# A hand-built instruction list for a convolution layer: a clock for all its DMA transfers, two late block loads held back, and the list built anew

## The chip, the cores and the metric

The kernel runs on one core of one Trainium2 chip. A core has a matrix engine (TensorE, PE in the profile, whose weight loads have a row of their own, PEld), a vector engine (VectorE, DVE), an activation engine (ScalarE, ACT), a general engine (GpSimd, POOL) and an engine that only issues DMA transfers (SyncE, SP). Each engine works off its own list of instructions in the order of the program, and the engines wait for one another by semaphores. The metric is the device time of one execution in microseconds (us): the median of several runs of the kernel before was 1088.61 us, from 1088.28 to 1089.37.

## The reference, cut to what matters

Two layers over 128 context tokens and 512 sample tokens (640 in all, width 1024), each `x + gate * mixer(modulated norm of x)`; shift, scale and gate come from a product of a condition vector with a large matrix (`ada_w`). Layer 0 is a convolution branch and layer 1 a state-space branch. The change concerns layer 0:

```python
m = jax.nn.silu(cond) @ w + b                       # shift, scale, gate of a layer
h = rms_norm(y, g) * (1.0 + sc) + sh
u = h @ w_in + b_in                                 # 1024 -> 3 * 2048
a, a_gate, z = jnp.split(u, 3, axis=-1)
v = a * jax.nn.sigmoid(a_gate)
v = depthwise_conv(v, w_dw, b_dw)                   # 31 taps along rows of 64
v = jax.nn.silu(layer_norm(v, ln_g, ln_b))
out = (v * jax.nn.silu(z)) @ w_out                  # 2048 -> 1024
y = y + gate * out
```

## The kernel before

**Tiles.** Channels lie on the 128 partitions and the 640 tokens along them. `u` has 48 tiles of 128 channels: 16 each of `a`, `g` (the gate) and `z`. One tile is 48 matmuls (three for each of 8 blocks of the inner dimension and each half of the tokens, since a float32 product is made from a high and a low part of both operands). `PLAN0` (line 42) gives the order in which PE makes the tiles after the opening, in which `g0`, `a0` and `g1` are made. Tile `i` of the convolution starts when `g i` has gone through the sigmoid on ACT (`after_g`, line 642) and `a i` has been multiplied with it on DVE (`after_a`, line 654) into `v i`, which lies in one of four buffers. PE's result lies in one of two PSUM buffers (`mm`), which come free when ACT or DVE has read them.

**The convolution** of a tile is 31 taps. `NPOOL[i]` (line 43) of them are multiplied by ACT (`late_taps`, line 828, into three buffers `tp`) and added by POOL (`seam_sums`, line 842); the centre tap is the first write of ACT (`init`, line 791); the rest run on DVE, one instruction a tap (`conv`, line 799). POOL also forms, by a product and four sums (lines 855 to 865), the tap products that cross the seam of the two token halves. When a tile is done, ACT squares it (`square`, line 699), and PE's column sums of tile and square go into the spare columns of the PSUM buffer of a later tile (`side_sums`, line 715), from where DVE adds them up (`add_sums`, line 727). After all 16 tiles come the statistics (`stats`, line 880, and `means`, line 896), the normalising on DVE (`normalise`, line 911), the gate (`gate_z`, line 923) and the products with `w_out` (`out_pass`, line 944).

**Weights.** Each tile needs 512 KB. SP loads them as `wf` (two buffers; `weights`, line 391); ACT rounds them into a high part `wh` and writes its negative into `wl` (`split`, line 402); a second load, issued by POOL, adds the weights from memory onto `wl` as it lands, so that `wl` is the low part. So each tile costs two transfers, one on SP's queue and one on POOL's. `wh` and `wl` have three buffers each.

**Late blocks.** Of the 24 blocks of the condition's matrix, 16 are loaded in the course of layer 0 (`blocks`, line 688): four transfers of 256 KB each, on SP. PE multiplies a block ahead of a certain `g` tile (its host) into spare columns of that tile's PSUM buffer (`lead_of`, line 634), ACT copies the row out behind the tile's sigmoid (`row_copy`, line 627), and PE turns it behind the matching `a` tile (`ada_turn`, line 129). Block 0 goes with `g2`, block 1 with `g3`. From block 2 on, a block waits until block `n - 2` has been multiplied.

**The list.** None of these orders is written by hand. While the program is built, the class `Order` (line 244) plays the layer through: every generator above is a chain of steps "engine, duration, instruction", every buffer a ring with the time at which it comes free. At each step it takes, over all chains and engines, the one that could begin first by its own clocks (ties go by the priorities of `PRIO0`, line 41, the lower first) and issues that instruction. The durations are constants in the code. So the clocks decide only the order on each engine; on the chip the semaphores decide the times, and an instruction whose input is later than the list believed holds up all that follow on its engine. In this class a load by SP counts as landed 4.2 us after its issue (`LATE`), the accumulating load by POOL 6.6 us after (line 430), and a block 2.5 us after the 4.2 (line 697), each as if nothing else were being moved. Only the opening's loads have a clock of the transfers, `clock[DM]` (line 441). Layer 1 has an `Order` of its own, with its own clocks that start at constants (line 1986).

The step that chooses, in short:

```python
t = max(self.clock[eng], ch[1] + wait, self.port if shared else -99.0)
load = 1.28 if table and table != self.table else 0.0
key = (t + 0.4 * load if len(ways) == 1 else ..., ch[2], ch[3])
```

`table` is the set of functions that ACT has loaded: the sigmoid and the silu need different ones, and a change costs 1.28 us.

Of the kernel before, what the change touches and what calls it, by code (L numbers as in the profile page):

```python
# [37 lines left out]
NCST0 = _n - NCST  # L38


PRIO0 = {"firsts": 7, "ada_chain": 5, "modulation0": 3, "sums0": 4, "square0": 7, "first_split": -7, "conv": 3, "after_a": -5, "after_g": -7, "init": -7, "late_taps": 1, "late_adds": 3, "seam": 2, "copied": -6, "after_z": -7, "weights": 7, "split": -4, "row": 1, "square": -2, "filler": 5, "blocks": -1, "add_sums": -2, "stats": -5, "means": 0, "normalise": -4, "gate_z": 6, "late_block": -5, "residual": -3, "half_residual": -1, "root": -1, "modulation": 5, "split_h": 0, "scales": 6}
PLAN0 = "a1 z0 g2 a2 g3 a3 g4 a4 g5 a5 g6 a6 g7 a7 g8 a8 g9 a9 g10 z1 z2 a10 z3 g11 a11 g12 a12 g13 a13 g14 z4 a14 g15 a15 z5 z6 z7 z8 z9 z10 z11 z12 z13 z14 z15"
NPOOL = (12, 6, 12, 6, 12, 12, 8, 12, 2, 8, 9, 8, 12, 4, 6, 8)
PRIO1 = {"low": -1, "x_after": 0, "filler": 5, "decay_half": -1, "decay_state": -1, "chain0": 1, "chain1": 1, "other_y": -3, "copy_y": -3, "split_y": 6, "groups": 3, "decays": 7, "norms": -7, "gate": -6, "products1": 5, "products0": -1, "residual0": -5, "final0": -5, "w_chain": 4, "time_steps": 2, "columns": -6, "logarithm": 6, "rows_out": 3, "ends_out": 3, "weights_out": -3, "first_steps": 1, "b_after": -6, "c_after": -3, "z_after": -2, "split": -5, "add_residual": -7, "out_weights": -1, "free_bc": -3, "final1": 1, "prompt": 4, "residual1": -3, "store": 4, "final_rest": -1}
PLAN1 = "z00 x21 x03 b0 c0 x02 z01 x13 b1 x10 x11 z02 x12 z03 x20 c1 x23 x33 c2 x32 x22 z10 z11 o00 o01 z12 x30 z13 b2 o02 o03 z20 b3 o10 x31 z21 o11 z22 z23 c3 o12 z30 o13 z31 z32 o20 z33 o21 o22 o23"
DONE0 = []
# [3 lines left out]
def trunk(ctx: ExitStack, tc: tile.TileContext, a: dict):  # L50
    nc = tc.nc
# [4 lines left out]
    V, S, G, T = nc.vector, nc.scalar, nc.gpsimd, nc.tensor  # L56
# [50 lines left out]
    def ada_load(l, b, wtile, nk):  # L107

        ws = []
        for k0 in range(0, KD, nk):  # L110
            w = wtile("wa")
            nc.sync.dma_start(out=w[:, 0 : nk * 256], in_=a["w_ada"][12 * l + b, :, k0 * 256 : (k0 + nk) * 256])
            ws += [w[:, k * 256 : k * 256 + 256] for k in range(nk)]
        return l, b, ws
# [127 lines left out]
    PE, ACT, VE, PO, SP, DM, VL, PD = range(8)  # L242

    class Order:
# [63 lines left out]
        def run(self, until=None):  # L308
            while self.chains:
                self.settle()  # L310
                if until in self.keys:
                    return
                best = None
                for ch in self.chains:
                    if ch[4][0] != "op":
                        continue
                    ways, bias = (*ch[4][1:], 0.0)[:2]
                    for n, (eng, dur, fn, table) in enumerate(ways):
                        shared = eng in (PO, VL)
                        eng = VE if eng == VL else PO if eng == PD else eng  # L320
                        wait = (self.lead if eng == PE else MARGIN[eng]) if ch[5] != eng else self.same[eng]
                        t = max(self.clock[eng], ch[1] + wait, self.port if shared else -99.0)
                        load = 1.28 if table and table != self.table else 0.0
                        key = (t + 0.4 * load if len(ways) == 1 else t + dur - ways[0][1] + bias * n, ch[2], ch[3])
                        if best is None or key < best[0]:
                            best = key, ch, eng, t + load, dur, fn, table, shared
                if best is None:
                    break
                _, ch, eng, t, dur, fn, table, shared = best
                if table:  # L330
                    self.table = table
                fn()
                self.clock[eng] = t + dur - OVER[eng]
                if shared:
                    self.port = t + dur - (0.2 if eng == PO else OVER[eng])
                ch[1] = t + dur + LATE.get(eng, 0.0)
                ch[5] = eng
                self.advance(ch, ch[1])
            assert not self.chains, [c_[4] for c_ in self.chains]
# [2 lines left out]
    OVER = {PE: 0.0, ACT: 0.1, VE: 0.08, PO: 0.04, SP: 0.0, DM: 0.0}  # L342
    LATE = {SP: 4.2}
    def op(eng, dur, fn, table=None):
        return "op", ((eng, dur, fn, table),)

    def either(*ways, bias=2.0):
        return "op", tuple((e_, d_, f_, None) for e_, d_, f_ in ways), bias
# [1 line left out]
    def key(*ks):  # L350
        return ("key",) + ks

    def get(name):
        return "get", name
# [23 lines left out]
    if True:  # L378
        run = Order(PRIO0)
        post, put, start = run.post, run.put, run.start  # L380
        for name, n in (("wf", 2), ("wh", 3), ("wl", 3), ("mm", 0), ("tm", 2), ("v", 4), ("cva", 2), ("cs", 33), ("tp", 3), ("pr", 1), ("eb", 3), ("hT", 0), ("hb", 0), ("sq", 1)):
            run.ring(name, n)
        plan = PLAN0.split()
        tiles0 = [{"a": 0, "g": 16, "z": 32}[n[0]] + int(n[1:]) for n in plan]
# [6 lines left out]
        def weights():  # L391
            src = [(("w", m), a["w_in1"][m]) for m in tiles0]
            for pi, nc_ in ((0, 4), (1, 8), (2, 4)):
                src += [(("out", pi, n), a[f"w_out1_{pi}"][n]) for n in range(nc_)]
            src += [(("l1", n), w) for n, w in enumerate((a["w_dt"], a["w_xbc"][0], a["w_xbc"][1]))]
            for name, w in src:
                yield get("wf")
                wf = gp.tile([P, 1024], F32, tag="wf", bufs=2, name="wf")
                t = yield op(SP, 0.35, lambda: nc.sync.dma_start(out=wf, in_=w))
                start(split(name, wf, w), t)  # L400

        def split(name, wf, src):
# [184 lines left out]
    with tc.tile_pool(name="l0", bufs=1) as lp:  # L587
# [6 lines left out]
        cv = [None] * 16  # L594

        eb = []
        for i in range(3):
            t = lp.tile([P, 2, 30], F32, name=f"eb{i}")
# [26 lines left out]
        sgs, vs = {}, {}  # L625
# [61 lines left out]

        def blocks():
            for n, (l, b) in enumerate(BLOCKS):
                if n > 1:  # L690
                    yield key(("ada", n - 2))
                for _ in range(4):
                    yield get("cs")
                blk = []
                t = yield op(SP, 1.8, lambda: blk.append(ada_load(l, b, cs, 2)))
                rows_[n] = blk
                post(("wa", n), t + 2.5)

# [85 lines left out]
        def rows64(t, lo, hi):  # L784
            return t.rearrange("p (r w) -> p r w", w=64)[:, :, lo:hi]
# [56 lines left out]
        def seam_sums(i):  # L842

            yield get("eb")
            e, v = eb[i % 3], vs[i]

            def edges():
                S.copy(out=e[:, 0, 14:29], in_=v[:, HN : HN + 15])
                S.copy(out=e[:, 1, 0:15], in_=v[:, 49:64])
            t = yield op(ACT, 0.31, edges)  # L850
            post(("eb", i), t)
            yield get("pr")
            pr = lp.tile([P, 2, 15, 15], F32, tag="pr", bufs=1, name="seam")

            def products():
                ea = e[:, :, :]
                win = bass.AP(tensor=ea.tensor, offset=ea.offset, ap=[list(ea.ap[0]), [30, 2], [1, 15], [1, 15]])
                wa = w_dw(i, 16)
                wv = bass.AP(tensor=wa.tensor, offset=wa.offset, ap=[list(wa.ap[0]), [-16, 2], [1, 15], [0, 15]])
                G.tensor_tensor(out=pr, in0=win, in1=wv, op=ALU.mult)  # L860
            t = yield op(PO, 1.04, products)
            put("eb", t)
            for a0, a1, n, d_ in ((0, 8, 7, 0.69), (0, 4, 4, 0.49), (0, 2, 2, 0.34), (0, 1, 1, 0.3)):
                yield op(PO, d_, lambda: G.tensor_add(out=pr[:, :, a0 : a0 + n, :], in0=pr[:, :, a0 : a0 + n, :], in1=pr[:, :, a1 : a1 + n, :]))
            yield key(("copied", i))

            def seam():
                oa = cv[i][:, 49:64]
                sm = bass.AP(tensor=oa.tensor, offset=oa.offset, ap=[list(oa.ap[0]), [HN - 49, 2], [1, 15]])
                G.tensor_add(out=sm, in0=sm, in1=pr[:, :, 0, :])  # L870
            t = yield op(PO, 0.3, seam)
            put("pr", t)
            for n, tap in enumerate(TAPS[:NPOOL[i]]):
                d, lo, hi = span_of(tap)
                yield key(("tp", i, n))
                t = yield op(PO, 1.28 + 0.0175 * (hi - lo - 49), lambda: G.tensor_add(out=rows64(cv[i], lo, hi), in0=rows64(cv[i], lo, hi), in1=sgs["tp", i, n][:, :, 0 : hi - lo]))  # L876
                put("tp", t)
            post(("cv" if i < 14 else "added", i), t)

# [292 lines left out]
    if True:  # L1172
# [8 lines left out]
        for i in range(2):  # L1181
            t = lp.tile([P, 646], F32, name=f"up{i}")
# [25 lines left out]
        xr, rp, e, q, t, u, v, one = (tr(n) for n in ("xr", "rp", "e", "q", "t", "u", "v", "one"))  # L1208
# [908 lines left out]
```

## Time and profile before

| what | us |
|---|---|
| median of 3 runs (lowest to highest) | 1088.61 (1088.28 to 1089.37) |
| the profiled execution | 1088.08 |
| its span, first to last instruction | 1086.3 |
| PE busy in the span | 1047.8 |
| DVE, ACT, POOL busy in the span | 795.1, 666.3, 456.4 |

The profile comes from one execution. Its views are a page (busy times, the span in 40 slices, DMA queues, the chain that ended last, groups of instructions) and answers to questions about the trace: waits by engine, instructions in order of time, busy times in given stretches. A row of the order in time reads: start, length, engine, line, operation, output<-inputs, and in brackets how long the engine was idle just before and what ended that. Several equal neighbours are merged into one row (x3). PSUM tiles of layer 0 are named by number in that view: `u__655`, `u__748`, `u__822`, `u__907` and `u__997` are the tiles a1, z0, g2, a2 and g3; `u__2593`, `u__2695` and `u__2798` are z1, z2 and a10; `u__4007` is a15. The instructions of layer 0's list run to about 555 us of the span; they take in the first products of layer 1 (L1040).

### The profile page before, as it was taken

To read this page: it belongs to the slowest core of one execution; us is meant where nothing else is said; L and a number is where in the kernel's file an instruction comes from. 1 tells how busy PE (TensorE), PEld (TensorE's weight loads), DVE (VectorE), ACT (ScalarE), POOL (GpSimd) and SP (SyncE) were. 2 spreads that over 40 slices of the span, in tenths; PEclk is the share of its full clock that TensorE was granted. 3 is DMA by queue.
4 is the path that set the end of the run, shared out by engine and by line. 5 is a ranking of instruction groups with operands and counts; after the bars stand their busy time and mean duration, and the time that the engine had idled before them with its cause. 6 is when DMAs were issued, how large, how long until landed. Compare 5 with 4: busy or idle time off the path is not lost. (4 is left out here: it accounts for less than half of the span.)

```text
span 1086.3 us, 19905 instructions
## 1 busy us (share of the span) xinstructions
PE 1047.8 (96%) x7888; PEld 976.3 (90%) x7888; DVE 795.1 (73%) x1188; ACT 666.3 (61%) x1093; POOL 456.4 (42%) x461
## 2 busy tenths in 40 slices
PE   6999999989999999999998999999999999999996
PEld 3898999989999999999998998988889988988895
DVE  2579999987999695103789597789777766776763
ACT  6457778878688686333576566585658353754442
POOL 0028989988599211111000145323531463364323
PEclk9999999999999999999999999999999999999997
DMA  9487787777755666676111635233341335343102
GB/s 362 181 227 190 205 214 180 183 206 209 189 124 135 138 144 152 150 163 130 59 63 66 160 87 136 69 108 98 107 117 64 102 107 127 91 105 107 40 20 97
DMA packets 86541, 146.94 MB, mean 135 GB/s; under 512 B 26928, under 2 KB 49840, under 8 KB 86448
## 3 DMA queue, kind: packets, MB, share of 16 engines
q1 hardware_dynamic: 77088, 113.91, 33.8%
q0 software_dynamic: 8640, 30.94, 16.3%
q8 instruction: 62, 1.02, 0.4%
q10 hardware_dynamic: 720, 0.82, 0.2%
q14 instruction: 31, 0.25, 0.1%
HBM read 140.73 MB, written 4.92 MB: 134 GB/s over the span
## 5 line engine op out<-in xcount | busy, mean ns | idle before, releaser
L804 DVE SCALAR_TENSOR_TENSOR cva<-v,cst,cva 128x620 f32<-128x620 f32 (+10 forms) x343 | 266.8, 823 | 16.3 <-ACT cva L796 11.8
L876 POOL TENSOR_TENSOR cv<-cv,tp 128x490 f32<-128x490 f32 (+5 forms) x137 | 174.9, 1276 | 10.1 <-ACT tp L835 1.2
L835 ACT ACTIVATE tp<-v,cst 128x490 f32<-128x490 f32 (+5 forms) x137 | 94.8, 719 | 41.6 <-POOL cv L876 41.2
L418 ACT CAST wh<-wf 128x1024 fp32r<-128x1024 f32 x63 | 65.9, 1045 | 67.9 <-PE o__5278 L155 29.9
L1239 ACT CAST wh<-wf 128x1024 fp32r<-128x1024 f32 x53 | 55.4, 1044 | 67.4 <-PE o L1277 25.6
L1277 PE MATMUL o<-yhl,wh 128*128 128x320 f32 x384 | 92.5, 328 | 0.0
L1277 PE MATMUL pz<-h_hi,wh 128*128 128x320 f32 x256 | 88.3, 345 | 1.3 <-ACT up L1308 1.3
L1243 DVE TENSOR_TENSOR wl<-wf,wh 128x1024 fp32r<-128x1024 f32 x48 | 66.2, 1379 | 31.5 <-ACT wh L1239 31.3
L1565 POOL TENSOR_TENSOR y<-y,yo 128x512 f32<-128x512 f32 x32 | 45.4, 1417 | 85.9 <-DVE yo L1563 82.6
L1277 PE MATMUL pz<-h_hi,wl 128*128 128x320 f32 x256 | 79.1, 309 | 0.0
L1277 PE MATMUL pz<-h_lo,wh 128*128 128x320 f32 x256 | 79.0, 309 | 0.0
L1277 PE MATMUL xs<-h_hi,wh 128*128 128x320 f32 x224 | 75.1, 335 | 0.0
L1321 DVE SCALAR_TENSOR_TENSOR xs<-up,cst,xs 128x642 f32<-128x642 f32 x64 | 66.1, 1032 | 7.4 <-PE ptx L1345 3.4
L1277 PEld LDWEIGHTS o<-yhl,wh 128*128 128x128 f32 x384 | 63.8, 188 | 7.5 <-issue 7.2
L1277 PE MATMUL xs<-h_lo,wh 128*128 128x320 f32 x224 | 69.9, 312 | 0.0
L1277 PE MATMUL xs<-h_hi,wl 128*128 128x320 f32 x224 | 69.9, 312 | 0.0
L429 POOL DMA_DIRECT2D wl<-w_in x43 | 37.4, 870 | 60.0 <-ACT wl L428 59.3
L428 ACT ACTIVATE wl<-wh 128x1024 fp32r<-128x1024 f32 x58 | 61.5, 1060 | 1.8
L1277 PE MATMUL o<-yhl,wl 128*128 128x320 f32 x192 | 59.4, 309 | 0.0
L1440 ACT ACTIVATE gf<-gf,cols 128x128 f32<-128x128 f32 x160 | 50.5, 391 | 8.5 <-DVE gf L1436 7.3
L1277 PEld LDWEIGHTS pz<-h_hi,wh 128*128 128x128 f32 x256 | 48.1, 188 | 7.2 <-issue 5.6
L1277 PEld LDWEIGHTS pz<-h_lo,wh 128*128 128x128 f32 x256 | 48.2, 188 | 3.8 <-issue 3.8
(842 smaller groups left out, 3379.3 us busy)
## 6 DMA issues: line engine op xcount, KB each, us to landing
wf<-w_in SPq DMA_DIRECT2D x48, 512.0 KB, 3.7
wl<-w_in POOLq DMA_DIRECT2D x43, 512.0 KB, 6.9
wa<-w_ada SPq DMA_DIRECT2D x64, 256.0 KB, 6.1
wf<-w_out SPq DMA_DIRECT2D x32, 512.0 KB, 3.7
wf<-w_xbc SPq DMA_DIRECT2D x24, 512.0 KB, 3.9
gf<-acd SPq DMA_DIRECT2D x40, 256.0 KB, 4.5
wa<-w_ada SPq DMA_DIRECT2D x16, 512.0 KB, 10.2
wf<-w_z SPq DMA_DIRECT2D x16, 512.0 KB, 3.7
```

Of the source, the lines that this page charges most:

```text
L418: t = yield op(ACT, 1.05, lambda: S.copy(out=wh, in_=wf))
L428: yield op(ACT, 1.06, lambda: S.activation(out=wl, in_=wh.bitcast(F32), func=AF.Copy, scale=-1.0))
L429: t = yield op(PD, 0.7, lambda: G.dma_start(out=wl, in_=src, accum_op=ALU.add))
L804: t = yield op(VE, 0.24 + 0.01 * (hi - lo), lambda: V.scalar_tensor_tensor(out=rows64(accs[i], lo, hi), in0=rows64(vs[i], lo + d, hi + d), ...
L835: t = yield op(ACT, 0.72, lambda: S.activation(out=tp[:, :, 0 : hi - lo], in_=rows64(vs[i], lo + d, hi + d), func=AF.Copy, scale=w_dw(i, t ...
L876: t = yield op(PO, 1.28 + 0.0175 * (hi - lo - 49), lambda: G.tensor_add(out=rows64(cv[i], lo, hi), in0=rows64(cv[i], lo, hi), in1=sgs["tp" ...
L1239: S.copy(out=cell["wh"], in_=cell["wf"])
L1243: e_.tensor_sub(out=cell["wl"], in0=cell["wf"], in1=cell["wh"].bitcast(F32))
L1277: T.matmul(ps[:, b, at_ : at_ + t1 - t0], lhsT=w_, rhs=t_[:, t0:t1], start=k == 0 and n == 0, stop=k == nk - 1 and n == 2)
L1321: t = yield op(VL, 0.89, lambda: V.scalar_tensor_tensor(out=acc, in0=u[:, d : d + PW], scalar=c("w_c", j * 5 + d), in1=acc, op0=ALU.mult, ...
L1440: t = yield op(ACT, 0.39, lambda: S.activation(out=gv[:, h_, :], in_=gv[:, h_, :], func=AF.Exp, bias=cols1[ch][:, o8 + h_ : o8 + h_ + 1]), ...
L1565: t = yield op(PO, 1.29, lambda: G.tensor_add(out=y, in0=y, in1=yo))
```

## The change

Five parts, all in the code that builds layer 0's list; no instruction of layer 0 changes its form.

1. **A clock for the transfers.** Every load of a tile's weights by SP now moves `clock[DM]` on by 1.55 us, a block by 3.1 and an accumulating load by 3.1 (`QUEUE`), and the step counts as landed no earlier than that clock says.
2. **Blocks 0 and 1 wait in the list**: block 0 for the weights of the first tile of the plan (a1), block 1 for those of the third (g2). Before, both could go at once after the opening.
3. **POOL's durations**: the seam's product from 1.04 to 1.09 us, its sums from 0.69, 0.49, 0.34 to 0.8, 0.56, 0.36, a tap from 1.28 + 0.0175 a column to 1.3 + 0.019.
4. **`NPOOL`**: tile 5 from 12 to 11 taps on ACT and POOL, tile 7 from 12 to 10; the others go to DVE.
5. **The order**: in `PLAN0` a15 comes two tiles later, behind z5 and z6; in `PRIO0` "row" goes from 1 to 5 and "means" from 0 to -3.

```diff
-PLAN0 = "a1 z0 g2 a2 g3 a3 g4 a4 g5 a5 g6 a6 g7 a7 g8 a8 g9 a9 g10 z1 z2 a10 z3 g11 a11 g12 a12 g13 a13 g14 z4 a14 g15 a15 z5 z6 z7 z8 z9 z10 z11 z12 z13 z14 z15"
-NPOOL = (12, 6, 12, 6, 12, 12, 8, 12, 2, 8, 9, 8, 12, 4, 6, 8)
+PLAN0 = "a1 z0 g2 a2 g3 a3 g4 a4 g5 a5 g6 a6 g7 a7 g8 a8 g9 a9 g10 z1 z2 a10 z3 g11 a11 g12 a12 g13 a13 g14 z4 a14 g15 z5 z6 a15 z7 z8 z9 z10 z11 z12 z13 z14 z15"
+NPOOL = (12, 6, 12, 6, 12, 11, 8, 10, 2, 8, 9, 8, 12, 4, 6, 8)
...
-                        load = 1.28 if table and table != self.table else 0.0
+                        load = 1.28 if table and eng == ACT and table != self.table else 0.0
...
-                if table:
+                if table and eng == ACT:
                     self.table = table
...
                 ch[1] = t + dur + LATE.get(eng, 0.0)
+                if table and eng != ACT:
+                    self.clock[DM] = max(self.clock[DM], t + 0.3) + table
+                    ch[1] = max(ch[1], self.clock[DM] + (2.2 if eng == SP else -3.6))
...
     def op(eng, dur, fn, table=None):
-        return "op", ((eng, dur, fn, table),)
+        return "op", ((eng, dur, fn, table or (QUEUE if eng == PD else None)),)
+    QUEUE = 3.1
...
-                t = yield op(SP, 0.35, lambda: nc.sync.dma_start(out=wf, in_=w))
+                t = yield op(SP, 0.35, lambda: nc.sync.dma_start(out=wf, in_=w), 1.55)
...
-                if n > 1:
-                    yield key(("ada", n - 2))
+                yield key(("ada", n - 2) if n > 1 else ("w", tiles0[2 * n]))
...
-                t = yield op(SP, 1.8, lambda: blk.append(ada_load(l, b, cs, 2)))
+                t = yield op(SP, 1.8, lambda: blk.append(ada_load(l, b, cs, 2)), 3.1)
...
-            t = yield op(PO, 1.04, products)
+            t = yield op(PO, 1.09, products)
...
-            for a0, a1, n, d_ in ((0, 8, 7, 0.69), (0, 4, 4, 0.49), (0, 2, 2, 0.34), (0, 1, 1, 0.3)):
+            for a0, a1, n, d_ in ((0, 8, 7, 0.8), (0, 4, 4, 0.56), (0, 2, 2, 0.36), (0, 1, 1, 0.3)):
...
-                t = yield op(PO, 1.28 + 0.0175 * (hi - lo - 49), ...)
+                t = yield op(PO, 1.3 + 0.019 * (hi - lo - 49), ...)
```

`PD` is POOL issuing an accumulating load; `table`, the fourth field of a step, now carries either ACT's set of functions or, on SP and POOL, the time that a transfer takes.

More of the change, by code (lines that the diff above doesn't have):

```diff
@@ L38 @@
 NCST0 = _n - NCST
-PRIO0 = {"firsts": 7, "ada_chain": 5, "modulation0": 3, "sums0": 4, "square0": 7, "first_split": -7, "conv": 3, "after_a": -5, "after_g": -7, "init": -7, "late_taps": 1, "late_adds": 3, "seam": 2, "copied": -6, "after_z": -7, "weights": 7, "split": -4, "row": 1, "square": -2, "filler": 5, "blocks": -1, "add_sums": -2, "stats": -5, "means": 0, "normalise": -4, "gate_z": 6, "late_block": -5, "residual": -3, "half_residual": -1, "root": -1, "modulation": 5, "split_h": 0, "scales": 6}
-PLAN0 = "a1 z0 g2 a2 g3 a3 g4 a4 g5 a5 g6 a6 g7 a7 g8 a8 g9 a9 g10 z1 z2 a10 z3 g11 a11 g12 a12 g13 a13 g14 z4 a14 g15 a15 z5 z6 z7 z8 z9 z10 z11 z12 z13 z14 z15"
-NPOOL = (12, 6, 12, 6, 12, 12, 8, 12, 2, 8, 9, 8, 12, 4, 6, 8)
+PRIO0 = {"firsts": 7, "ada_chain": 5, "modulation0": 3, "sums0": 4, "square0": 7, "first_split": -7, "conv": 3, "after_a": -5, "after_g": -7, "init": -7, "late_taps": 1, "late_adds": 3, "seam": 2, "copied": -6, "after_z": -7, "weights": 7, "split": -4, "row": 5, "square": -2, "filler": 5, "blocks": -1, "add_sums": -2, "stats": -5, "means": -3, "normalise": -4, "gate_z": 6, "late_block": -5, "residual": -3, "half_residual": -1, "root": -1, "modulation": 5, "split_h": 0, "scales": 6}
+PLAN0 = "a1 z0 g2 a2 g3 a3 g4 a4 g5 a5 g6 a6 g7 a7 g8 a8 g9 a9 g10 z1 z2 a10 z3 g11 a11 g12 a12 g13 a13 g14 z4 a14 g15 z5 z6 a15 z7 z8 z9 z10 z11 z12 z13 z14 z15"
+NPOOL = (12, 6, 12, 6, 12, 11, 8, 10, 2, 8, 9, 8, 12, 4, 6, 8)
 PRIO1 = {"low": -1, "x_after": 0, "filler": 5, "decay_half": -1, "decay_state": -1, "chain0": 1, "chain1": 1, "other_y": -3, "copy_y": -3, "split_y": 6, "groups": 3, "decays": 7, "norms": -7, "gate": -6, "products1": 5, "products0": -1, "residual0": -5, "final0": -5, "w_chain": 4, "time_steps": 2, "columns": -6, "logarithm": 6, "rows_out": 3, "ends_out": 3, "weights_out": -3, "first_steps": 1, "b_after": -6, "c_after": -3, "z_after": -2, "split": -5, "add_residual": -7, "out_weights": -1, "free_bc": -3, "final1": 1, "prompt": 4, "residual1": -3, "store": 4, "final_rest": -1}
@@ L875, in seam_sums @@
                 yield key(("tp", i, n))
-                t = yield op(PO, 1.28 + 0.0175 * (hi - lo - 49), lambda: G.tensor_add(out=rows64(cv[i], lo, hi), in0=rows64(cv[i], lo, hi), in1=sgs["tp", i, n][:, :, 0 : hi - lo]))
+                t = yield op(PO, 1.3 + 0.019 * (hi - lo - 49), lambda: G.tensor_add(out=rows64(cv[i], lo, hi), in0=rows64(cv[i], lo, hi), in1=sgs["tp", i, n][:, :, 0 : hi - lo]))
                 put("tp", t)
```

## The prediction

> **What bounds the kernel now.** I read the page first, then PE's waits in layer 0 after the opening, then busy times by stretch, then the order in time around each wait.
>
> ```profile
> span 1086.3 us, 19905 instructions
> PE 1047.8 (96%) x7888; PEld 976.3 (90%) x7888; DVE 795.1 (73%) x1188; ACT 666.3 (61%) x1093; POOL 456.4 (42%) x461
> ```
>
> PE is the bound: 96% of the span, and the change takes no matmul away. Only PE's idle time, and time at a lower clock, can be won. The waits of PE from 54 us (end of the opening's products) to 555 us (end of layer 0's list) are these; the columns are total, times, longest:
>
> ```profile
> PE u__2798 L619 <- DVE ssum L730: 3.9, 1, 3.9
> PE u__907 L130 <- ACT ada_row L630: 2.2, 1, 2.2
> PE u__907 L619 <- DMA wl<-w_in: 1.2, 1, 1.2
> PE u__4007 L130 <- ACT ada_row L630: 0.4, 1, 0.4
> PE dt L1040 <- DVE h_lo L1120: 0.2, 1, 0.2
> ```
>
> So 7.9 us of idle, nearly all in two places: tile a2 (1.2 + 2.2 = 3.4 us) and tile a10 (3.9 us). Busy time by stretch (PE, PEld, DVE, ACT, POOL, then clock, DMA share, GB/s):
>
> ```profile
> 54.00:70.00 16.00, 15.93 (x132) 15.43 (x132) 9.50 (x12) 7.16 (x12) 3.91 (x9) 1.00 0.76 230
> 70.00:90.00 20.00, 16.66 (x137) 15.91 (x136) 18.53 (x25) 13.18 (x18) 7.04 (x8) 1.00 0.81 211
> 90.00:222.00 132.00, 132.00 (x1187) 129.93 (x1186) 129.65 (x184) 105.27 (x163) 123.25 (x132) 1.00 0.76 192
> 222.00:240.00 18.00, 14.13 (x124) 13.62 (x123) 14.79 (x22) 15.12 (x22) 14.10 (x20) 0.91 0.81 211
> ```
>
> The granted clock is 1.00 around the waits of 1.2 and 2.2 us, and 0.91 over the 18 us with the wait of 3.9: another (1 - 0.91) x 18 = 1.6 us. [...] All that can be won is 7.9 + 1.6 = 9.5 us. The opening and layer 1 keep their lists: the opening's loads had their clock already, and layer 1's `Order` starts from constants.
>
> **The first wait, at a2.** SP, ACT, DVE, ACT and PE in order of time:
>
> ```profile
> 54.13 3.65 SPq L112 DMA_DIRECT2D wa<-w_ada  x8
> 57.88 14.88 SPq L399 DMA_DIRECT2D wf<-w_in  x4
> ...
> 68.31 1.05 ACT L418 CAST wh<-wf 128x1024 fp32r<-128x1024 f32 x1 [8.81 <-DMA wf<-w_in]
> ...
> 63.23 2.55 DVE L804 SCALAR_TENSOR_TENSOR cva<-v,cst,cva 128x580 f32<-128x580 f32 x3
> 71.26 19.00 DVE L804 SCALAR_TENSOR_TENSOR cva<-v,cst,cva 128x520 f32<-128x520 f32 x25 [5.48 <-ACT cva L796]
> ...
> 84.42 0.69 ACT L811 COPY cv<-cva 128x640 f32<-128x640 f32 x1 [5.61 <-DVE cva L804]
> 85.13 1.28 ACT L646 ACT_TABLE_LOAD   x1
> 86.42 0.79 ACT L646 ACTIVATE sg<-u__822,cst 128x640 f32<-128x640 f32 x1
> 87.11 0.26 ACT L630 COPY ada_row<-u__822 128x128 f32<-128x128 f32 x1
> ...
> 78.24 0.41 PE L619 MATMUL u__907<-h_hi,wl 128*128 128x320 f32 x1 [1.17 <-DMA wl<-w_in]
> 87.42 0.39 PE L130 MATMUL u__907<-cst,ada_row 128*128 128x4 f32 x2 [2.17 <-ACT ada_row L630]
> ```
>
> One chain: at 54.13 both blocks go out on SP (8 transfers of 256 KB), the weights of a2 only at 57.88, behind them. ACT stands 8.81 us at the head of its list for those weights, while the `init` of tile 1 waits behind it; DVE runs dry for 5.48 us; tile 0 is finished that much later, and its copy on ACT (waiting 5.61 us) stands ahead of g2's sigmoid and row copy, for which PE then waits.
>
> The change leaves block 0 where it is (a1's weights are there long before) and puts block 1 behind g2's arrival, so behind the weights of a2. That takes 4 x 256 KB = 1.05 MB out of the way of a2's weights: 3.1 us at the highest rate seen there, 4.6 us at the mean of 54 to 70 us (230 GB/s).
>
> ```profile
> 66.00:68.00 2.00, 2.00 (x16) 2.00 (x15) 0.00 (x0) 0.00 (x0) 0.00 (x0) 1.00 0.85 334
> ...
> DMA to landing us min/median/max: 7.4/8.6/10.5
> ```
>
> (The first row is a stretch of 2 us, at 334 GB/s; the second the accumulating loads `wl` of 50 to 100 us.) ACT's cast of a2 moves from 68.31 to 63.7 to 65.2, DVE's idle time from 5.48 to 0.9 to 2.4, the end of the row copy from 87.37 to 82.8 to 84.3. PE wants it at 87.42 - 2.17 = 85.25, or at 84.1 once the wait of 1.17 is gone. So even with the old order on ACT the 2.2 us shrink to 0 to 0.2. The 1.2 us depend on `wl` of a2: earlier by 3.1 to 4.6 it has 1.9 to 3.4 us to spare. Block 1 now shares the engines with just that load: with the slowest landing of that row in place of the fastest (10.5 for 7.4) it loses 3.1, and could wait up to 1.2 again. I take it as gone: **3.4 us**, bounds 2.0 and 3.4. [...]
>
> **The second wait, at a10.** ACT, DVE and PE:
>
> ```profile
> 219.39 0.75 ACT L835 ACTIVATE tp<-v,cst 128x530 f32<-128x530 f32 x1 [1.48 <-POOL cv L876]
> ...
> 224.17 1.28 ACT L675 ACT_TABLE_LOAD   x1
> 225.46 0.79 ACT L675 ACTIVATE sz<-u__2593,cst 128x640 f32<-128x640 f32 x1
> ...
> 226.29 0.49 DVE L730 TENSOR_TENSOR ssum<-ssum,u__2593 128x320 f32<-128x320 f32 x1 [1.80 <-ACT sz L675]
> ...
> 222.65 0.31 PE L619 MATMUL u__2695<-h_hi,wl 128*128 128x320 f32 x1
> 226.83 0.50 PE L619 MATMUL u__2798<-h_hi,wh 128*128 128x320 f32 x1 [3.87 <-DVE ssum L730]
> ```
>
> PE is done with z2 at 222.96 and needs the buffer of z1, whose silu and sum come only at 225.46 and 226.29. The silu needs another table, so the list puts it behind every other ready step of ACT until it sees a gap of over 0.4 x 1.28 = 0.5 us. There was one, 1.48 us before 219.39, spent waiting for POOL; the list did not see it because its POOL was too quick:
>
> ```profile
> L876 POOL TENSOR_TENSOR cv<-cv,tp 128x490 f32<-128x490 f32 (+5 forms) x137 | 174.9, 1276 | 10.1 <-ACT tp L835 1.2
> L804 DVE SCALAR_TENSOR_TENSOR cva<-v,cst,cva 128x620 f32<-128x620 f32 (+10 forms) x343 | 266.8, 823 | 16.3 <-ACT cva L796 11.8
> L864 POOL TENSOR_TENSOR seam<-seam 128x210 f32<-128x210 f32 (+1 forms) x64 | 28.3, 442 | 3.9
> ```
>
> The four seam sums take 28.3/16 = 1.77 us; the old constants make 1.82 - 4 x 0.04 (overlap) = 1.66, the new 1.86. With about 0.025 a tap and 0.25 a seam more, the new clock of POOL is 90 x 0.025 + 10 x 0.25 = 4.8 us later after ten tiles (90 taps). A list that sees the gap puts table and silu at 217.9, ends them at 220.0, and the sum can follow on DVE before 222.96. That would win 3.9 + 1.6 = **5.5 us**. Bounds: 0 (the silu stays where it is) and 5.5. I take 5.5, since the gap of 1.48 lies well over the 0.5 needed.
>
> **The rest.** Three taps move to DVE: 3 x 266.8/343 = 2.3 us there, 3 x 1.28 = 3.8 off POOL. [...] a15 two tiles later:
>
> ```profile
> 61.33 0.31 PE L619 MATMUL u__748<-h_hi,wh 128*128 128x320 f32 x1
> 68.46 1.08 PE L639 MATMUL u__822<-wa,scz 128*32 128x128 f32 x32
> ...
> 421.90 1.75 DVE L936 TENSOR_TENSOR y_lo<-sz,y_hi 128x640 fp32r<-128x640 f32 x2
> 439.22 0.31 PE L155 MATMUL o__4996<-y_hi,wh 128*128 128x320 f32 x1
> ```
>
> A tile is 7.1 us on PE (61.33 to 68.46), so v15 comes 14.2 us later against PE's work. The last `y` is ready at 423.65 and first needed at 439.22: 15.6 us of slack, so that even if everything behind v15 moved with it, 1.4 us stay. "means" only swaps two steps in front of that slack; "row" is the name of no chain. Cost: nothing, up to 1 us if the slack is overdrawn.
>
> A list that is built anew has waits of its own. The trace cannot show them; bounds are 0 and 9.5 (what the old list left). I take 2.5, one more wait of the kind of 2.2 and some tenths, because from 90 to 222 us, the fullest stretch of all engines, the old list had none.
>
> **Sum** against the profiled execution: 1088.08 - 3.4 - 5.5 + 2.5 = 1081.7. The median of the runs lies 0.5 above that execution: 1082.2.
>
> **Rivals.**
> 1. *One of the two waits stays.* The silu still falls behind the taps, or block 0 alone keeps a2's weights late. For it: the order of tiles around z1 is the same, and so are the two buffers. Against it: the gap, and the arithmetic above. Gain 3.4 or 5.5 less 1 to 2.5 of new waits: 1084 to 1087.
> 2. *The change doesn't do what it says: the wait only moves.* POOL is busy 123.25 of 132 us; if POOL and ACT set the date of z1's silu, PE comes to a10 3.4 us earlier and waits 3.4 longer. Gain 0 to 2: 1087 to 1088.6.
> [...]
>
> **How the numbers follow.** Forecast 0.47 (own range 1079.5 to 1084.5), rival 1 0.25, rival 2 0.15, rival 3 0.13. The range 1079.0 to 1090.5 reaches from all 9.5 us won to rival 2 with the bounds of new waits; rival 3 lies mostly outside. About 0.2% (2.2 us) can be told from no change: faster takes the forecast and 0.22 of rival 1, 0.69; within 0.18; slower 0.13.
>
> **What would show it.** Right: only block 0's four transfers ahead of a2's weights on SP; ACT's wait there under 5 us; no PE wait at a2; z1's silu within 5 us of its last matmul, and a clock of 1.00 at 222 to 240 us. Wrong: new PE waits of over 5 us in sum between 90 and 360, DVE idle at 66 to 71 as before, or a wait of PE for `y` after z15.

## The result, and the profile after

The changed kernel takes 1078.73 us (median of 4 runs, 1078.34 to 1079.58), the kernel before 1088.99 us in the same session (4 runs, 1088.28 to 1090.38): a ratio of 0.9905, 95% interval 0.9888 to 0.9922. The forecast was 1082.2 us with a range of 1079.0 to 1090.5: right in sign, 3.5 us too high, and the time lies 0.3 us below the range. The profiled execution took 1079.03 us.

The head of the page of the changed kernel (busy time, share of the span, instructions):

```profile
span 1077.2 us, 19904 instructions
PE 1044.6 (97%) x7888; PEld 974.8 (90%) x7888; DVE 798.7 (74%) x1191; ACT 664.6 (62%) x1090; POOL 451.6 (42%) x458
```

PE's waits from 54 to 555 us, the same view as before (total, times, longest):

```profile
PE pz L1280 <- ACT up L1311: 1.3, 1, 1.3
PE dt L1043 <- DVE h_lo L1123: 0.2, 1, 0.2
```

Both are in layer 1; that of `pz` was there before too, behind the end of the window. In layer 0 nothing is left after the opening. Busy time by stretch (PE, PEld, DVE, ACT, POOL, granted clock, DMA share, GB/s):

```profile
70.00:90.00 20.00, 20.00 (x182) 19.59 (x171) 19.75 (x28) 15.10 (x20) 10.18 (x11) 1.00 0.93 269
90.00:222.00 132.00, 132.00 (x1186) 129.81 (x1186) 130.20 (x185) 107.32 (x165) 123.02 (x134) 1.00 0.81 198
222.00:240.00 18.00, 18.00 (x186) 17.37 (x186) 17.54 (x26) 12.91 (x21) 12.61 (x16) 1.00 0.79 200
```

PE is busy 20.00 of 20 us where it was 16.66, and 18.00 of 18 at clock 1.00 where it was 14.13 at 0.91. The order in time around the old first wait (SP, ACT, DVE, ACT):

```profile
55.17 1.75 SPq L112 DMA_DIRECT2D wa<-w_ada  x4
57.03 8.57 SPq L403 DMA_DIRECT2D wf<-w_in  x3
65.64 2.05 SPq L112 DMA_DIRECT2D wa<-w_ada  x4
...
64.19 1.05 ACT L422 CAST wh<-wf 128x1024 fp32r<-128x1024 f32 x1 [3.66 <-DMA wf<-w_in]
...
67.14 19.01 DVE L807 SCALAR_TENSOR_TENSOR cva<-v,cst,cva 128x520 f32<-128x520 f32 x25 [0.33 <-ACT cva L799]
...
83.01 0.26 ACT L634 COPY ada_row<-u__822 128x128 f32<-128x128 f32 x1
```

Block 1 now stands on SP behind the weights of a2, g3 and a3. ACT waits 3.66 us for a2's weights instead of 8.81, DVE 0.33 instead of 5.48, and the row of g2 is copied in time. Around the old second wait (ACT, DVE, PE; the tiles z1, z2 and a10 are `u__2588`, `u__2689` and `u__2794` here):

```profile
212.29 0.73 ACT L838 ACTIVATE tp<-v,cst 128x520 f32<-128x520 f32 x1 [1.50 <-POOL cv L879]
212.92 1.03 ACT L422 CAST wh<-wf 128x1024 fp32r<-128x1024 f32 x1
213.99 1.06 ACT L432 ACTIVATE wl<-wh 128x1024 fp32r<-128x1024 f32 x1
214.96 2.20 ACT L838 ACTIVATE tp<-v,cst 128x530 f32<-128x530 f32 x3
217.17 1.28 ACT L679 ACT_TABLE_LOAD   x1
218.47 0.79 ACT L679 ACTIVATE sz<-u__2588,cst 128x640 f32<-128x640 f32 x1
...
219.44 0.48 DVE L733 TENSOR_TENSOR ssum<-ssum,u__2588 128x320 f32<-128x320 f32 x1
...
55.21 0.41 PE L623 MATMUL u__655<-h_hi,wh 128*128 128x320 f32 x1
219.98 0.41 PE L623 MATMUL u__2794<-h_hi,wh 128*128 128x320 f32 x1
```

The gap of 1.5 us is still there, and behind it stand the same steps as before: cast, `wl`, three taps, table, silu. The list does not use the gap. All of it only comes earlier: a10 begins 164.77 us after a1 (219.98 - 55.21), before 172.65 (226.83 - 54.18).

So that runs with different openings can be compared, I take the start of every tile's first matmul, count it from a1's first, and subtract the same number of the changed kernel. What a kernel is late at some tile, in us:

```
                                        g3     a10      z3     a11   z8 to z15
before                                3.87    7.89    9.43    9.43   10.0
```

That splits the gain: 3.87 at a2, 4.02 at a10, 1.54 more while a10 runs at a lower clock (granted 0.91 from 222 to 240 us, 1.00 in the changed kernel), 0.57 around a15: 10.0 us. In these two profiles the opening takes 1.03 back (a1 starts at 55.21 instead of 54.18); 10.0 - 1.03 is the 9.05 between the profiled executions to within 0.1.

### The profile page after: what moved, and what is told of

Read it like the earlier page. It is cut to its first block, busy times and chain, and to the rows that moved or that the text cites. A ratio compares the mean times of both kernels' runs of the same rounds, so it can differ in the third digit from the quotient of the medians.

```text
span 1077.2 us, 19904 instructions
## 1 busy us (share of the span) xinstructions
PE 1044.6 (97%) x7888; PEld 974.8 (90%) x7888; DVE 798.7 (74%) x1191; ACT 664.6 (62%) x1090; POOL 451.6 (42%) x458
## 5 line engine op out<-in xcount | busy, mean ns | idle before, releaser
L807 DVE SCALAR_TENSOR_TENSOR cva<-v,cst,cva 128x550 f32<-128x550 f32 (+12 forms) x346 | 270.2, 822 | 11.6 <-ACT cva L799 6.5
L879 POOL TENSOR_TENSOR cv<-cv,tp 128x490 f32<-128x490 f32 (+5 forms) x134 | 172.7, 1289 | 8.5
L838 ACT ACTIVATE tp<-v,cst 128x490 f32<-128x490 f32 (+5 forms) x134 | 92.4, 718 | 35.9 <-POOL cv L879 35.6
```

The costliest lines, as they stand in the source:

```text
L807: t = yield op(VE, 0.24 + 0.01 * (hi - lo), lambda: V.scalar_tensor_tensor(out=rows64(accs[i], lo, hi), in0=rows64(vs[i], lo + d, hi + d), ...
L838: t = yield op(ACT, 0.72, lambda: S.activation(out=tp[:, :, 0 : hi - lo], in_=rows64(vs[i], lo + d, hi + d), func=AF.Copy, scale=w_dw(i, t ...
L879: t = yield op(PO, 1.3 + 0.019 * (hi - lo - 49), lambda: G.tensor_add(out=rows64(cv[i], lo, hi), in0=rows64(cv[i], lo, hi), in1=sgs["tp", ...
```

## The experiments

Theory 'late' says that an engine which the list believes too early comes late to a step for which PE waits; it and its rivals stand in the expectations. All ratios are against the kernel before in the same session. The table continues the one above, and is referred to below:

```
                                        g3     a10      z3     a11   z8 to z15
E1  old list, block 1 later           0.01    2.72    3.27    4.05    4.70
E7  clock alone                      -0.01    2.65    4.19    4.19    4.78
E10 hold alone                        0.00    2.85    4.38    4.38    5.07
E9  POOL's durations alone            3.19    4.67    4.98    6.19    6.09
E5  E1 and silu ahead                -0.01    0.68    7.00    7.00    7.63
E6  old list, block 1 later + POOL   -0.01   -0.04    0.06    1.25    1.15
E12 parts 1 to 3                      0.01   -0.02    0.06    1.23    1.12
E2  new list, block 1 first           5.06    5.49    5.39    5.39    5.39
E3  new without POOL's durations     -0.01    3.69    5.23    5.23    5.23
E4  new without the tap counts       -0.01   -0.04    0.22    1.38    1.38
E8  new without PLAN0 and PRIO0       0.06    0.73    0.73    0.73    0.63
E11 new without the clock             0.00   -0.02   -0.09   -0.09   -0.09
```

**E1: the old order on every engine, only block 1 later.** In block 1's place the data of block 2 are loaded, in transfers of the same size.

```diff
-                t = yield op(SP, 1.8, lambda: blk.append(ada_load(l, b, cs, 2)))
+                t = yield op(SP, 1.8, load if n != 1 else lambda: held.append(load))
...
                 t = yield op(SP, 0.35, lambda: nc.sync.dma_start(out=wf, in_=w))
+                if held and name == ("w", tiles0[5]):
+                    held.pop()()
```

> The list of before, every engine's order unchanged, except that the four transfers of block 1 go out on SP behind three tile loads instead of ahead of them. Prediction's view (two separate waits): the waits at a2 (1.2 + 2.2 us) go, the wait at a10 (3.9 us, clock 0.91) stays: about 3.4 us faster, 1085.6. Rival, one cause: ACT's standing wait for a2's weights falls from 8.8 to about 3.7, so the other engines win some 5.1 us and PE 3.4; the wait at a10 shrinks by the difference of 1.7 to about 2.2, short enough that the clock stays at 1.00: 3.4 + 1.7 + 1.6 = 6.7 us faster, 1082.3. Rival, the wait moves: PE waits 3.4 us longer at a10, no gain, 1089.

1084.17 us, ratio 0.9948 (0.9933 to 0.9963). PE's waits in E1:

```profile
PE u__2798 L623 <- DVE ssum L736: 2.6, 1, 2.6
...
PE u__2902 L130 <- ACT ada_row L634: 0.5, 1, 0.5
PE u__4007 L130 <- ACT ada_row L634: 0.5, 1, 0.5
PE u__2695 L130 <- ACT ada_row L634: 0.3, 1, 0.3
```

Four transfers moved on one queue take the whole wait at a2 away, with no other order changed. And the wait at a10 falls from 3.9 to 2.6 instead of growing: 1.3 us of it was the first stall, still felt some 135 us later by ACT, which had not caught up. That is the rival of one cause in kind: the wait shrinks and the granted clock stays at 1.00. It had 2.2 us and 1082.3; the time lies between that and the prediction's 1085.6.

**E2: the new list, block 1's four transfers put straight behind block 0's.**

```diff
+                    blk.append(early.pop() if n == 1 else ada_load(l, b, cs, 2))
+                    if n == 0:
+                        early.append(ada_load(*BLOCKS[1], cs, 2))
```

> The list of after, every engine's order unchanged, except that block 1's four transfers go out on SP right behind block 0's, ahead of a2's weights. Prediction's view: the waits at a2 come back, nothing at a10: 3.4 us slower than after, 1082.1. [...]

1084.37 us, ratio 0.9949 (0.9932 to 0.9965). PE waits at a2 again (columns as above), and ACT stands idle for 8.92 us ahead of the cast of a2's weights:

```profile
PE u__907 L130 <- ACT ada_row L634: 2.9, 1, 2.9
...
PE u__907 L623 <- DMA wl<-w_in: 0.6, 1, 0.6
```

The wait costs 5.06 us by g3 and 5.51 one tile on, 1.6 more than before, because the clock fell behind it (0.53 from 88 to 90 us, 0.62 from 90 to 92). At a10 there is no wait, and nothing more is lost behind z1 (5.51 there, 5.39 at z3). So the time lies 2.3 us above the 1082.1 of the prediction's view, and most of that is the lower clock behind the wait at a2.

**E3: the new list with POOL's old durations.**

```diff
-            t = yield op(PO, 1.09, products)
+            t = yield op(PO, 1.04, products)
...
-            for a0, a1, n, d_ in ((0, 8, 7, 0.8), (0, 4, 4, 0.56), (0, 2, 2, 0.36), (0, 1, 1, 0.3)):
+            for a0, a1, n, d_ in ((0, 8, 7, 0.69), (0, 4, 4, 0.49), (0, 2, 2, 0.34), (0, 1, 1, 0.3)):
...
-                t = yield op(PO, 1.3 + 0.019 * (hi - lo - 49), ...)
+                t = yield op(PO, 1.28 + 0.0175 * (hi - lo - 49), ...)
```

> The change without its third part: POOL's durations in the list are the old ones, all else as after. Prediction's view: z1's silu falls behind taps whose end the list believes too early and the wait at a10 comes back, 3.9 us and 1.6 of clock: 1084.2. Rival: those constants are not what removed the wait; the order around z1 is as in after, no wait over 1 us, 1078.7.

1084.18 us, ratio 0.9946 (0.9931 to 0.9961). The wait at a10 is back, with its fall of the clock (0.91 from 222 to 240 us, as before), and a2 stays clean:

```profile
PE u__2795 L623 <- DVE ssum L733: 3.6, 1, 3.6
```

**E4: the new kernel with the old tap counts.**

```diff
-NPOOL = (12, 6, 12, 6, 12, 11, 8, 10, 2, 8, 9, 8, 12, 4, 6, 8)
+NPOOL = (12, 6, 12, 6, 12, 12, 8, 12, 2, 8, 9, 8, 12, 4, 6, 8)
```

> The change without its fourth part: 12 taps of tiles 5 and 7 on ACT and POOL again, all else as after. Prediction's view: the taps cost PE nothing, 1078.7, within 1 us. Rival, POOL's load sets the date of z1's silu: 3 taps are 3.8 us of POOL ahead of z1, the margin at a10 was 0.1 us, so PE waits about 3.7 us there and the clock may fall (1.6): 1082.4 to 1084.

1081.11 us, ratio 0.9921 (0.9906 to 0.9935). One new wait, for the row that ACT copies out of z3's buffer:

```profile
PE u__2903 L130 <- ACT ada_row L634: 0.9, 1, 0.9
```

It costs 1.16 us at a11 (0.22 to 1.38). Three taps more for DVE take it away: they cost nothing, they win 1.4 us. Neither expectation had this: the taps are worth something, and not at a10.

**E5: E1 (with block 1's own data), and z1's silu run ahead of the three taps that stood before it on ACT.** `c_` is the chain of z1; its silu is issued ahead of the tap `fn`, and its own step then issues nothing. This is the prediction's second term done by hand in the old list.

```diff
+                if self.prio is PRIO0 and ch[0].gi_code.co_name == "late_taps":
...
+                            if len(early) == 1:
+                                e_, d_, f_, n_ = c_[4][1][0]
+                                f_()
+                                c_[4] = "op", ((e_, d_, lambda: None, n_),)
                 fn()
```

> The list of before, every engine's order kept but for two edits: block 1's four transfers go on SP behind the third tile load after block 0 (as in E1, here with block 1's own data), and the silu of z1 stands on ACT ahead of the three late taps behind which it stood, with its table load. Theory 'late': what is left at a10 in E1 (2.6 us) is only ACT coming to z1's silu too late; the three taps ahead of it took 2.2 us and 1.3 us of table load stay, so the silu ends about 2.1 us earlier, the wait of PE at a10 falls from 2.6 to about 0.5, and the time from E1's 1084.2 to about 1082.1 (1081.6 to 1083.0). The three taps come 2.1 us later; if these are what PE waits for next (the row of a block, or the squares of a convolution tile), the gain comes back behind a10 and the time stays at 1083.5 to 1084.5. Theory 'DVE': the wait at a10 is DVE's sum being behind other work of DVE (28 taps without a gap), not ACT's silu: wait at a10 stays at 2.0 to 2.6 and the time at 1083.6 to 1084.6.

1085.39 us, ratio 0.9972 (0.9960 to 0.9985): not faster than E1. PE's waits, and its busy time by stretch:

```profile
PE u__2695 L130 <- ACT ada_row L644: 3.1, 1, 3.1
...
PE u__2798 L633 <- DVE ssum L746: 0.6, 1, 0.6
```

```profile
224.00:228.00 4.00, 0.93 (x5) 0.77 (x4) 2.35 (x5) 3.30 (x6) 2.54 (x5) 0.88 0.65 136
228.00:232.00 4.00, 4.00 (x16) 4.00 (x16) 3.86 (x6) 1.93 (x4) 2.33 (x4) 0.50 0.64 152
```

The wait at a10 falls from 2.6 to 0.6, as expected. But ACT is late with everything, and what stood behind the silu is now later against PE: the row of z2, 3.1 us, and the clock at 0.50 behind it. Between a10 and z3 this loses 6.3 us (0.68 to 7.00), and the time lies above every range expected, none of which had a fall of the clock. Moving the instruction that PE waits for only names the next one.

**E6: the old list, block 1 later, and POOL's durations of part 3.** No clock, old tap counts and orders. Beside the edit of E1 (with block 1's own data) and the other two lines of part 3:

```diff
-            t = yield op(PO, 1.04, products)
+            t = yield op(PO, 1.09, products)
```

> The list of before with block 1 on SP behind the third tile load (as E1, with its own data) and, besides, POOL's durations as in the change; no clock of the transfers, the old tap counts, PLAN0 and PRIO0. Theory 'late': the two corrections that matter are these two, so PE's waits at a2 and at a10 are both gone (each below 0.6 us) and the time is 1080.0 to 1082.0, E4's 1081.1 within it, since only tap counts and order are then missing. Theory 'the list must be rebuilt with the clock of the transfers': the wait at a10 stays at 1.5 to 2.6 us as in E1 and the time at 1083.0 to 1084.8. In both the wait at a2 is below 0.3 us.

1080.43 us, ratio 0.9930 (0.9915 to 0.9944). Neither old wait is there; the one left in layer 0 is E4's, 0.9 us for z3's row.

So two corrections in the old list, a place on one queue and a handful of constants, bring 8.85 of the 10.0 us.

**E7: part 1 alone, the clock of the transfers** (its other lines are those of the change):

```diff
+                if table and eng != ACT:
+                    self.clock[DM] = max(self.clock[DM], t + 0.3) + table
+                    ch[1] = max(ch[1], self.clock[DM] + (2.2 if eng == SP else -3.6))
```

> Part 1 of the change alone: the clock of the transfers, with blocks 0 and 1 not held, POOL's old durations, tap counts and orders. In this list block 1 stands on SP behind one tile load (that of a2), the other loads behind it. Theory 'late': the clock alone already takes the wait at a2 away (below 0.5 us; before 3.3) and leaves the one at a10, since POOL's steps are still believed too short: 2.6 to 3.9 us there as in E1 and E3, time 1083.5 to 1085.5. Rival 'the hold of part 2 does it': without the hold a wait of 2 us or more stays at a2 or g3 and the time is 1085.5 to 1088.5.

1084.34 us, ratio 0.9964 (0.9952 to 0.9976). SP's queue in E7:

```profile
55.88 0.36 SPq L403 DMA_DIRECT2D wf<-w_in  x1
56.29 2.88 SPq L112 DMA_DIRECT2D wa<-w_ada  x4
59.26 12.17 SPq L403 DMA_DIRECT2D wf<-w_in  x3
```

The clock alone lets a2's weights go ahead of block 1 (the four `wa` at 56.29); that suffices. At a10 remain 2.5 us:

```profile
PE u__2798 L623 <- DVE ssum L734: 2.5, 1, 2.5
```

**E8: the changed kernel with the old `PLAN0` and `PRIO0`** (of `PLAN0` only the end of the list differs, of `PRIO0` "row" 1 and "means" 0).

```diff
-... g15 z5 z6 a15 z7 ...
+... g15 a15 z5 z6 z7 ...
```

> The changed kernel with PLAN0 and PRIO0 as before (a15 two tiles earlier, 'row' 1, 'means' 0); clock, hold, POOL's durations and tap counts as changed. Theory 'late': the order is worth only the small wait at a15 (0.4 us before, tiles 0.57 us later), so the time is 0.3 to 0.9 us above the changed kernel: 1079.0 to 1079.8, with a wait of 0.3 to 0.6 us at a15. Rival 'the order was searched for this list and carries a part of the gain': a new wait of 1 us or more somewhere between a2 and a15, time 1080.3 to 1083.

1079.87 us, ratio 0.9921 (0.9905 to 0.9936). By the times it can't be told from the changed kernel; by tiles it is 0.63 us behind. The wait is at a10, not at a15:

```profile
PE u__2794 L623 <- DVE ssum L733: 0.5, 1, 0.5
```

**E9: part 3 alone, POOL's durations (the diff of E3 the other way round, in the kernel before), block 1 ahead of a2's weights.** With before, E1 and E6 this is the fourth corner.

> Part 3 alone in the list of before: POOL's durations; block 1 stays ahead of a2's weights. With before (neither), E1 (block 1 later alone) and E6 (both) this is the fourth corner. Theory 'two causes that add up': the waits at a2 stay (3.3 us recorded, 3.9 in the tiles), the one at a10 is gone (below 0.8 us) with its clock fall, and the time is before's less what E6 is below E1 (3.7): 1084 to 1086. Theory 'one lateness': the wait at a10 is mainly inherited from the stall at a2, so it stays at 1.5 us or more as long as that stall stays, and the time is 1086.5 to 1088.5.

1086.17 us, ratio 0.9978 (0.9968 to 0.9989). PE's waits in E9:

```profile
PE u__907 L130 <- ACT ada_row L630: 1.4, 1, 1.4
...
PE u__2792 L619 <- DVE ssum L730: 1.3, 1, 1.3
PE u__907 L619 <- DMA wl<-w_in: 1.2, 1, 1.2
PE u__2903 L130 <- ACT ada_row L630: 0.9, 1, 0.9
```

Neither theory had the wait right: 1.3 us at a10 lies between "below 0.8" and "1.5 or more", and the time 0.2 above the first one's range. The four corners give the answer: 3.9 us (before), 2.6 (block 1 later), 1.3 (POOL's durations), none (both). The wait at a10 was 1.3 us inherited from a2 and 2.6 us from POOL's durations, and they add up. From 222 to 240 us the granted clock was 0.91 with the 3.9 us of before, and 1.00 with E1's 2.6; in E9, with 1.3, it was 1.00 in every stretch read from 80 to 240 us.

**E10: part 2 alone, the hold.**

```diff
-                if n > 1:
-                    yield key(("ada", n - 2))
+                yield key(("ada", n - 2) if n > 1 else ("w", tiles0[2 * n]))
```

> Part 2 alone: blocks 0 and 1 wait in the list for the weights of a1 and g2; no clock of the transfers, POOL's old durations, tap counts and orders. In this list block 1 stands on SP behind three tile loads, as in the changed kernel. Theory 'late': the same as E1 and E7, since all that counts is block 1 behind a2's weights: no wait at a2, 2.5 us left at a10, time 1083.5 to 1085.0. Rival 'the hold needs the clock' (later loads are believed too early and a tile of weights comes late): a wait for wl of over 1 us appears, time 1085.5 to 1088.5.

1084.11 us, ratio 0.9957 (0.9944 to 0.9970), with 2.7 us left at a10:

```profile
PE u__2798 L619 <- DVE ssum L729: 2.7, 1, 2.7
```

**E11: the changed kernel without part 1** (the diff of part 1 taken back).

> The changed kernel without part 1: no clock of the transfers; hold, POOL's durations, tap counts and orders as changed. Theory 'late': the hold alone already puts block 1 behind a2's weights, and POOL's durations keep the list on time, so the clock adds nothing or little: 1078.5 to 1080.2, no wait over 0.6 us in layer 0. Rival 'the clock is what keeps the list on time': a wait of over 1 us for weights or behind them, time 1080.5 to 1084.

1078.83 us, ratio 0.9911 (0.9897 to 0.9926), as the changed kernel. At a2 clock and hold do the same thing: either suffices in the old list (E7, E10), and the hold does in the new one.

**E12: parts 1 to 3 of the diff, with the old tap counts, `PLAN0` and `PRIO0`.**

> Parts 1 to 3 of the change (clock, hold, POOL's durations) with the old tap counts, PLAN0 and PRIO0: what the corrected times give before anything is searched anew. Theory 'late': as E6, 1080.0 to 1081.2, with the wait of 0.9 us for a block's row behind a10 that E4 and E6 show, and 0.3 to 0.6 us at a15; the search (parts 4 and 5) is then worth 1.3 to 2 us. Rival 'the old orders do not fit the corrected list': a wait of 2 us or more, 1082 to 1086.

1081.29 us, ratio 0.9927 (0.9907 to 0.9947), 0.1 above the range given; by tiles the same as E6: parts 4 and 5 are worth 1.1 us together. The wait at a15 that I had expected here and in E8 is not there: after z3 neither loses anything (1.23 to 1.12, 0.73 to 0.63), while E7 and E10, with POOL's old durations, still lose 0.6 to 0.7 at a15.

No run beats the changed kernel (E11 equals it), and in layer 0 it leaves PE no wait to take away.

## Why the prediction was right in direction and too high

**Term 1, the wait at a2: the mechanism was right, the size 0.5 too small.** Only block 0 stands ahead, ACT's wait is under 5 us, the row copy ends at 83.27, inside the 82.8 to 84.3 given. Since a1 itself began 1.03 later, the weights came earlier than I had worked out: counted from a1, ACT's cast of a2 moved by 5.15 us (14.13 to 8.98), not by 3.1 to 4.6. E1, E2, E7 and E10 show the cause: whichever way block 1 gets behind a2's weights, the wait is gone, and putting it back brings it back. The size was 3.4 and is 3.87. The rest can be read from the rows of before:

```profile
76.76 0.31 PE L619 MATMUL u__907<-h_lo,wh 128*128 128x320 f32 x1
78.24 0.41 PE L619 MATMUL u__907<-h_hi,wl 128*128 128x320 f32 x1 [1.17 <-DMA wl<-w_in]
78.49 0.31 PE L619 MATMUL u__907<-h_hi,wh 128*128 128x320 f32 x1
78.64 0.30 PE L619 MATMUL u__907<-h_lo,wh 128*128 128x320 f32 x1
```

A matmul is recorded as 0.31 us, but without a wait the next one begins 0.15 after it; behind the wait the first takes 0.25. From 76.76 to 78.49 are 1.73 us in place of 0.29: 1.44 lost, where 1.17 is recorded as idle. The wait for the row, recorded as 2.17, makes up the other 2.43.

The bound of 2.0 supposed that the `wl` of a2 lands more slowly once block 1 is behind a2's weights, and so it did. That one load's landing, in before (first row) and after (second):

```profile
wl<-w_in POOLq DMA_DIRECT2D x1, 512.0 KB, 7.4
```

```profile
wl<-w_in POOLq DMA_DIRECT2D x1, 512.0 KB, 10.3
```

With block 1 ahead of a2's weights it took 6.7 to 8.2 us (before, E2, E9), with block 1 behind them 8.4 to 10.7 (the other eleven kernels). Other loads ran beside it too, so block 1's own share is not shown. PE does not wait for it, because it is issued 5.15 us earlier, counted from a1 (66.64 - 55.21 for 70.76 - 54.18): it lands at 76.94, 1.0 us before the first matmul that needs it, at 77.94.

**Term 2, the wait at a10: the size was right (5.5 given, 4.02 + 1.54 measured), the mechanism wrong.** The silu was not put into the gap: the gap and the order around it are unchanged, and the silu starts 7.1 us after z1's last matmul, where I had said within 5. That the size came out all the same is luck: whatever brings the silu in time wins the same wait and clock. What the durations change is which taps stand ahead of it. Counting ACT's taps (`late_taps`) up to z1's silu gives 80 in before, E1, E3, E7 and E10, the lists with POOL's old durations, and 78 in E2, E4, E6, E8, E9, E11, E12 and the changed kernel, those with the new. Lists with equal tap counts compare: before with E9, E1 with E6, E3 with the changed kernel. ACT can write a tap only as fast as POOL frees the three buffers (ACT's 1.50 us of idle at 212.29 ends with POOL's `cv`), and POOL is nearly always at work there (in the changed kernel 123.02 of 132 us from 90 to 222):

```profile
204.25 4.95 POOL L879 TENSOR_TENSOR cv<-cv,tp 128x490 f32<-128x490 f32 x4
209.16 0.98 POOL L863 TENSOR_TENSOR seam<-eb,cst 128x450 f32<-128x450 f32 x1
210.07 0.86 POOL L433 DMA_DIRECT2D wl<-w_in  x1
210.68 5.72 POOL L879 TENSOR_TENSOR cv<-cv,tp 128x510 f32<-128x510 f32 x4
```

Four taps in 5.72 us: two are 2.9, and from E1 to E6 the silu comes 2.99 us earlier against a1 (166.12 to 163.13). That POOL's durations do it is shown by the runs; that it goes by these two taps is worked out from the rows, no run moves them alone. a10 can begin 1.36 us after the silu starts: at 164.49 after a1 in E6, before PE itself comes to it at 164.73; at 167.48 in E1, which is the 2.72 of the table. I had also taken the two waits for separate; 1.3 of the 3.9 us came from the first (E1, E9).

**Term 3, new waits of the rebuilt list: this is the step that failed, 2.5 given, 0 measured.** The worry itself was sound: E12, the rebuilt list with the old tap counts and order, has its own wait of 0.9 us for z3's row, 1.2 in the tiles, 1.1 at the end. The new tap counts remove it (it is back in E4), but with the old order they bring 0.7 at a10 (E8), which the new order removes. I judged the rebuilt list by what the old one had left, and did not work out what parts 4 and 5 do to it: three taps and a tile's place take its waits away.

**"All that can be won is 9.5 us": 10.0 were won**, for the 0.5 of term 1. That bound carried the low end of the range (1088.6 - 9.5 = 1079.1), so the time could fall below it. The sum in the profiled times was 2.7 us too high: 2.5 of term 3, 0.5 of term 1, 0.1 of term 2, 0.6 at a15, costed at nothing, less 1.0 by which the opening was slower. The other 0.8 lie between profile and median: I added 0.5, and the profile after lies 0.3 above its median.

**The rivals.** Rival 1 (one wait stays, 1084 to 1087) is what each half of the change gives: E1, E2, E3, E7, E10 at 1084.1 to 1084.4. Rival 2 (the wait only moves) falls with E1: PE came to a10 3.87 us earlier and waited 1.3 less. Rival 3 (DVE becomes the bound, slower) falls with E4: the taps on DVE win 1.4 us. The later a15 delays the last `y`, and PE still does not wait for it.

## What to carry to other kernels

Where a list is built from durations, an engine that is a little slower than its constant makes everything behind it late, and the wait shows far away, at a step that has nothing to do with it; correct the constant and rebuild before moving the instruction that is waited for, since a late engine is late with the next thing too (E5). Follow a stall to what stood at the head of a queue when it began: four transfers in the wrong place cost 3.87 us here, with no engine's work changed. And count a stall by the start of the next tiles, not by the idle time recorded: what the record of a stall leaves out (0.26 us each at a2) and the clock (1.54 us behind a10 in the kernel before) came on top here.

## What was not expected of the hardware

- **The clock behind waits of 2.2 to 2.7 us.** The granted clock over the 18 us around a10, in E1 after a wait of 2.6 us and in E10 after one of 2.7:

```profile
222.00:240.00 18.00, 17.14 (x168) 16.45 (x172) 16.40 (x24) 13.45 (x23) 14.04 (x20) 1.00 0.84 212
```

```profile
222.00:240.00 18.00, 17.27 (x145) 17.03 (x146) 16.24 (x23) 13.72 (x23) 14.04 (x20) 0.91 0.85 208
```

  It also fell after the 2.5 us of E7 (0.91 in the same 18 us), and not after the 2.2 at a2 before (1.00 from 70 to 90 us). So of three waits of 2.5 to 2.7 us two were followed by a fall and one was not. What a fall cost here goes from 1.5 us (E7 and E10 between a10 and z3; E1, without one, loses 0.55 there) to 3.2 us (E5, where the granted clock of these 18 us is 0.81 and not 0.91: about twice the time at a clock of 0.50). How short a wait has to be to keep the clock, these runs do not show.
- **The opening varies.** Up to a1 the engines run the same instructions in the same order in all 14 profiles, yet a1 began anywhere from 54.06 us (E7) to 56.24 (E12). This alone is 2.2 us between profiles, twice what parts 4 and 5 are worth, and the reason for comparing tiles from a1 on.
